# Gated rows by seven products, and lent weight sums, in a two-layer encoder kernel

## The chip, the core and the metric

One core of a Trainium2 chip. The metric is the device time of one execution in microseconds, as the median of several. PE is TensorE, DVE VectorE, ACT ScalarE, POOL GpSimd, SP SyncE; DMA queues are fed by SP and POOL.

## The reference

One inference step of an encoder for a prompt of 512 frames and 8 streams of 16 frames, so 640 tokens, in fp32, with two layers. Each layer is an FFN at half weight, a mixer, and a second FFN:

```
x += 1/2 * SwiGLU_1(RMSNorm(x))
h  = RMSNorm(x);  z = h @ w_in          # conv B | C | V | q | k | v | 2 x 1024 gates
y_c = B * causal_conv3(C * V);  y_a = band attention of q, k, v
m = sigmoid(g_c) * (y_c @ w_conv_out) + sigmoid(g_a) * (y_a @ w_attn_out);  x += m @ w_o
x += 1/2 * SwiGLU_2(RMSNorm(x))
```

The change touches the line with m: y_c and y_a have 512 channels, the gates and m 1024.

## The kernel before

Tokens lie in the free dimension (640, as two halves t1 and t2 of 320), features in partitions, 128 rows at a time. Each fp32 operand is split in a high and a low part (`hi`, `lo`), and a product takes three matmuls per 128 rows: weights hi by x hi, hi by x lo, lo by x hi. ACT makes the high part by a cast, DVE the low one by a subtraction.

**By seven.** Where a weight block of 2 by 2 meets two halves of tokens, seven products are made in place of eight. A *unit* has two weight tiles `ra` and `rb` of 128 x 1024 (n and n + 1 of the stream `wst`) and takes four *slabs* from them, each split into `whi` and `wlo`: the first is `ra` (products 11 and 21), the second a sum `s6` and a sum of `rb`'s halves (N6 and T5), the third sums (T7 and 22), the fourth `rb`'s second half (T4). A product is 12 matmuls of 320 columns. The operands N6, T7, T4 and T5 are sums of the x quarters.

**The stretch.** `outputs` makes, per layer, the gates m = 2 to 15 in pairs (`gate_pair`: one unit for two rows of 128, with banks `qa`, `qb`, `qc`), and the products with `w_conv_out` ("co") and `w_attn_out` ("ao"). Of the latter, the rows 0 to 3 of each are made one by one (`out`: 24 matmuls into `py`), the rows 4 to 7 as one unit (`rows`, banks `ra`, `rb`, `rc`). `mixer_order` gives the order: gates 2, co 0 to 3, gates 4 and 6, co rows 4 to 7, gates 8, ao 0 and 1, gates 10, ao 2 and 3, gates 12 and 14, ao rows 4 to 7, then w_o. PE, DVE and ACT run there in the order in which the code is written.

**Gates.** A gate is scaled by the norm's `rr` (DVE), goes through the sigmoid (ACT), and is multiplied with its output (DVE). `mm` holds the co part and, after the ao part is added, m, which is split for w_o (`m_0hi`, `m_0lo`).

**Lent sums.** `lend_one` lets POOL's queue make a sum in memory: a transfer of half a tile, then a second one that adds. In the units of `lean` (from the third unit of the stretch on) it stands in for a DVE addition.

**Order of preparation.** `prep` makes the casts of a slab on ACT and notes its subtractions, `flush` issues them on DVE, `slab` and `quiet` take the next slab, `ahead` makes the sums of the slab after. There are three buffers for `whi` and three for `wlo`.

Of the kernel before, what the change touches and what calls it, by code (L numbers as in the profile page):

```python
# [194 lines left out]
def trunk(ctx: ExitStack, tc: tile.TileContext, xin, wst, small, pbias, samplebias, kcache, vcache, gfin,  # L197
# [80 lines left out]
    def lend_one(n):  # L278

        z = lent[n] = apart[0].tile([P, CH // 2], F32, tag="one", name=f"one{n}", bufs=2)  # L280
        POOL.dma_start(z, wst[n][:, h1])
        POOL.dma_start(z, wst[n + 1][:, h1], accum_op=ALU.add)
# [19 lines left out]
    def source(i):  # L302
# [3 lines left out]
        if i not in sources:  # L306
# [8 lines left out]
            else:  # L315
# [35 lines left out]
    def prep(i):  # L351
# [8 lines left out]
        o = 0  # L360
        for src, c in parts:
            d = slice(o, o + c.stop - c.start)
            o = d.stop
# [3 lines left out]
    def flush():  # L367
        for lo, src, hi in pending:
            DVE.tensor_tensor(out=lo, in0=src, in1=hi.bitcast(F32), op=ALU.subtract)  # L369
        pending.clear()  # L370
# [3 lines left out]
    def slab(hold=False):  # L374
# [10 lines left out]
        return ready[i], slabs[i]  # L385

# [1110 lines left out]
    def outputs(l, gp, X, st, cs, ycp, yas, sigmoid, gates):  # L1497
# [4 lines left out]
        ycs = [z[:, i] for z in ycp for i in range(2)]  # L1502
        mm = [spare[i // 2][:, i % 2] for i in range(CT)] + ycs
# [7 lines left out]
        lates = []  # L1511

        def due():
            for f in lates:
                f()
            lates.clear()

        def gate_pair(m, at):
            n = f"{l}_{m}"
            pa, pb, pc = (att(f"q{i}{n}")[:, :HT] for i in "abc")  # L1520
            s0 = quiet()
            block(pa, s0, 0, X11, every, True, True)
            ACT.copy(c1, pa)
            due()
            u, g = gates[m], gates[m + 1] = tmp(f"g{n}"), tmp(f"g{n}_1")
            prep(used[0] + 1)
            flush()
            at[0]()
            block(pb, s0, 1, X21, every, True, True)
            add(u[:, t1], pb, c1)  # L1530
            s1 = slab(True)[0]
            flush()
            block(pa, s1, 0, XN6, every, False, True)
            ACT.copy(u2, pa)
            block(pc, s1, 1, XT5, every, True, True)
            ACT.copy(c5, pc)
            at[1]()
            s2 = slab(True)[0]
# [4 lines left out]
            ahead()  # L1543
            at[2]()
            block(pc, s2, 1, X22, every, False, True)
            add(u[:, t2], pc, u2)
            s3 = slab(True)[0]
            DVE.tensor_tensor(out=u, in0=u, in1=rr, op=ALU.mult)
            lates.append(lambda: sigmoid(u, m))
            if m == 2:  # L1550
                for i in range(2):
                    sigmoid(gates[i], i)
            block(pa, s3, 0, XT4, every, False, True)
            DVE.tensor_tensor(out=g[:, t1], in0=pa, in1=rr[:, t1], op=ALU.mult)
            lates.append(lambda: sigmoid(g, m + 1, -1.0))
            flush()

        def parts(pool, tag, name, src):
            hi, lo = (pool.tile([P, T], F32R, tag=f"{tag}{i}", name=f"{name}{i}") for i in ("hi", "lo"))
            split(hi, lo, src)  # L1560
            return hi, lo

        def out(m, y, then=None, post=None):

            due()
            py = acc(f"py{l}_{m}")
            product(py, y)
            if then:
                then()
            g = gates[m]  # L1570
            if m < KT:
                DVE.tensor_tensor(out=halves(mm[m]), in0=two(py), in1=halves(g), op=ALU.mult)
            else:
                DVE.tensor_tensor(out=halves(g), in0=two(py), in1=halves(g), op=ALU.mult)
                add(mm[m - KT], mm[m - KT], g)
            flush()
            if post:
                post()

        yc, ya = [], []  # L1580
        mo = [None] * KT
        srcs = [yas[:, c, :] for c in range(CT)]
        x, moves = {}, []

        def take(y, name, cs, srcs):
            for c in cs:
                y.append(parts(gp, f"y{c}", f"{name}{l}_{c}", srcs[c]))

        def take_even(c):
            y = tuple(gp.tile([P, T], F32R, tag=f"y{c}{i}", name=f"ya{l}_{c}{i}") for i in ("hi", "lo"))  # L1590
            split(*(z[:, t1] for z in y), srcs[c][:, t1])
            ya.append(y)

        def low(lo, z, hi):
            DVE.tensor_tensor(out=lo, in0=z, in1=hi.bitcast(F32), op=ALU.subtract)

        def room(name):
            for k in EXTRA:
                x[name, k] = tuple(gp.tile([P, 2, HT], F32R, tag=f"x{EXTRA.index(k)}{i}",
                                           name=f"x{i}{name}{l}_{EXTRA.index(k)}") for i in ("hi", "lo"))  # L1600

        def minus(out, a):
            DVE.scalar_tensor_tensor(out=out, in0=a, scalar=-1.0, in1=out, op0=ALU.mult, op1=ALU.subtract)

        def mixed(i):

            z = ycp[i].rearrange("p c (a b) -> p (c a) b", a=2)
            e1, e2, o1, o2 = (z[:, k] for k in range(4))
            add(e1, e1, e2, ALU.subtract)
            add(e2, o2, e2, ALU.subtract)  # L1610
            minus(o2, e1)
            minus(o1, o2)
            yield
            for k in EXTRA:
                ACT.copy(x["co", k][0][:, i], z[:, 1 + EXTRA.index(k)])
            yield
            for k in EXTRA:
                hi, lo = (u[:, i] for u in x["co", k])
                low(lo, z[:, 1 + EXTRA.index(k)], hi)
            yield  # L1620
            hi, lo = (u[:, t2] for u in yc[2 * i])
            ACT.copy(hi, e1)
            yield
            low(lo, e1, hi)
            yield

        za = yas.rearrange("p (i c) (a b) -> p i (c a) b", i=2, a=2)

        def mix(n):

            e1, e2, o1, o2 = (za[:, :, k] for k in range(4))
            if n == 0:
                add(e1, e1, e2, ALU.subtract)
            elif n == 1:
                add(e2, o2, e2, ALU.subtract)
            else:
                minus(*((o2, e1) if n == 2 else (o1, o2)))

        def place(k):
            if k == XT5:  # L1640
                return [(*(u[:, t2] for u in ya[2 * i]), za[:, i, 0]) for i in range(2)]
            return [(*x["ao", k], za[:, :, 1 + EXTRA.index(k)])]

        def high(*ks):
            for k in ks:
                for hi, _, z in place(k):
                    ACT.copy(hi, z)

        def rest(*ks):
            for k in ks:  # L1650
                for hi, lo, z in place(k):
                    low(lo, z, hi)

        EXTRA = XT7, XT4, XN6

        def kind(name, i, k):
            if k in EXTRA:
                return tuple(z[:, i] for z in x[name, k])
            hi, lo = (yc if name == "co" else ya)[2 * i + (k in (X21, X22))]
            return tuple(z[:, t2 if k in (X22, XT5) else t1] for z in (hi, lo))  # L1660

        def rows(name, ms, first, mid=None, late=None, end=False, defer=False):

            n = f"{name}{l}_{ms[0]}"
            gs = [gates[m + (KT if name == "ao" else 0)] for m in ms]
# [3 lines left out]
            s1, s2, s5 = stage  # L1669

            def mul(ps, s, half, k, start):
                for u in range(2):
                    for i in range(2):
                        kp = half * NP + 2 * u + i
                        wh, wl = (z[:, kp * P : (kp + 1) * P] for z in s)
                        xh, xl = kind(name, i, k)
# [13 lines left out]
            def moved(r):  # L1690
                for u in range(2):
                    ACT.copy(mm[ms[2 * r + u]], gs[2 * r + u])

            w = quiet()
            mul(a, w, 0, X11, True)
            ACT.copy(s1, two(A))
            due()
            prep(used[0] + 1)
            flush()
            if first:  # L1700
                first()
            mul(b, w, 1, X21, True)
            add(s1, two(B), s1)
            w = slab(True)[0]
            flush()
            mul(a, w, 0, XN6, False)
            ACT.copy(s2, two(A))
# [731 lines left out]
```

## Time and profile before

| what | value |
|---|---|
| median of 3 runs | 2482.03 us (2480.78 to 2482.44) |
| span of the profiled execution | 2479.9 us, 2.1 us below that median |
| busy in the span | PE 99%, DVE 88%, ACT 56%, POOL 13% |
| the stretch of gates and outputs, layer 0 | 635.0 to 774.3 us |
| the same, layer 1 | 1863.5 to 2002.8 us |

The time of an execution is the span from the first to the last instruction and what lies around it. The span of 2479.9 us is that of the profiled execution; no other time of its own is on the page, so the median stands beside it. In a row of the profile, a line, an engine, an operation, and "out<-in" name the tiles with their numbers left out; a row of groups ends with its busy time, the mean of one in ns, and the engine's idle time just before with its cause. In a row of the timeline, the start and the duration come first.

### The profile page before, as it was taken

How to read it: one execution, taken by the hardware profiler on the slowest of the kernel's cores; microseconds unless marked ns; L12 is line 12 of the kernel's file. 1: busy time of each engine (PE TensorE's matmuls, PEld its weight loads, DVE VectorE, ACT ScalarE, POOL GpSimd, SP SyncE). 2: the span in 40 equal slices, each digit the busy share in tenths (PEclk: the TensorE clock that was granted, in tenths of full speed). 3: DMA queues.
4: the chain of work that ended last, by engine and by line, in shares of the span. 5: the costliest groups of instructions: out<-in, count | busy, mean ns of one | idle time of the engine just before them, and what ended most of it. 6: DMA issues, size and time to landing. Idle time of an engine off the chain costs nothing.

```text
span 2479.9 us, 44056 instructions
## 1 busy us (share of the span) xinstructions
PE 2466.4 (99%) x17264; PEld 2414.6 (97%) x17264; DVE 2182.6 (88%) x3644; ACT 1386.7 (56%) x2231; POOL 320.8 (13%) x483
## 2 busy tenths in 40 slices
PE   9999999999999999999999999999999999999999
PEld 8999999889999999999999999998899999999998
DVE  7999998888888899998799999988888889999997
ACT  6555555665555555555665555566655556555555
POOL 0211112211000001111001010121110000111111
PEclk9999999999999999999999999999999999999999
DMA  4443444335344234444334343452453432444444
GB/s 155 128 120 101 124 117 120 114 110 175 102 118 123 93 102 107 112 118 119 109 94 109 110 117 102 117 128 102 138 167 94 119 119 92 108 113 107 112 117 117
DMA packets 113520, 288.16 MB, mean 116 GB/s; under 512 B 12992, under 2 KB 52544, under 8 KB 113312
## 3 DMA queue, kind: packets, MB, share of 16 engines
q1 hardware_dynamic: 69552, 220.10, 27.0%
q0 software_dynamic: 43328, 64.99, 13.8%
q8 instruction: 135, 2.21, 0.4%
q14 instruction: 73, 0.60, 0.1%
q10 hardware_dynamic: 432, 0.25, 0.0%
HBM read 239.48 MB, written 7.94 MB: 100 GB/s over the span
## 4 chain that ended last, share of the span: by engine, by line
PE 91%; DVE 4%; issue 3%; ACT 1%; DMA 1%; DVEq 0%; SPq 0%; ACTq 0%; POOLq 0%
PE pab L459 12%; PE paa L459 10%; PE pcb L459 6%; PE daa L1147 5%; PE dab L1147 5%; PE pca L459 5%; PE po L435 5%; PE qa L459 4%; PE pbb L459 3%; PE dca L1147 3%; PE dcb L1147 2%; PE pba L459 2%; PE ma_cv L459 2%; PE ma_qk L459 2%; PE py L435 2%
## 5 line engine op out<-in xcount | busy, mean ns | idle before, releaser
L364 ACT CAST whi<-raw 128x1024 fp32r<-128x1024 f32 (+1 forms) x578 | 502.3, 874 | 373.4 <-PE pbb L459 46.3
L369 DVE TENSOR_TENSOR wlo<-raw,whi 128x1024 fp32r<-128x1024 f32 (+1 forms) x578 | 577.0, 1001 | 135.4 <-ACT whi L364 131.2
L364 ACT CAST whi<-s 128x1024 fp32r<-128x1024 f32 (+1 forms) x162 | 152.9, 944 | 319.4 <-DVE s L296 113.5
L459 PE MATMUL pab<-xhib,whi 128*128 128x320 f32 x704 | 217.7, 309 | 0.0
L459 PE MATMUL pab<-xhib,wlo 128*128 128x320 f32 x704 | 217.2, 309 | 0.0
L459 PE MATMUL pab<-xlob,whi 128*128 128x320 f32 x704 | 217.2, 309 | 0.0
L459 PE MATMUL paa<-xhia,whi 128*128 128x320 f32 x640 | 197.8, 309 | 0.2 <-DVE ga L296 0.2
L459 PE MATMUL paa<-xhia,wlo 128*128 128x320 f32 x640 | 197.5, 309 | 0.0
L459 PE MATMUL paa<-xloa,whi 128*128 128x320 f32 x640 | 197.5, 309 | 0.0
L369 DVE TENSOR_TENSOR wlo<-s,whi 128x1024 fp32r<-128x1024 f32 (+1 forms) x162 | 176.3, 1088 | 4.0 <-ACT whi L364 4.0
L1169 POOL DMA_DIRECT2D x<-c_a x80 | 69.9, 1021 | 575.9 <-ACT ahia L1051 205.5
L1169 POOL DMA_DIRECT2D x<-c_b x72 | 63.2, 1014 | 583.1 <-ACT ahib L1051 205.4
L459 PEld LDWEIGHTS pab<-xhib,whi 128*128 128x128 f32 x704 | 132.1, 188 | 0.9 <-issue 0.9
L459 PEld LDWEIGHTS pab<-xhib,wlo 128*128 128x128 f32 x704 | 132.1, 188 | 0.0
L459 PEld LDWEIGHTS pab<-xlob,whi 128*128 128x128 f32 x704 | 132.1, 188 | 0.0
L459 PEld LDWEIGHTS paa<-xhia,whi 128*128 128x128 f32 x640 | 120.1, 188 | 1.1 <-DVE ga L296 0.4
L459 PEld LDWEIGHTS paa<-xloa,whi 128*128 128x128 f32 x640 | 120.1, 188 | 0.3 <-DVE xloa L703 0.3
L459 PEld LDWEIGHTS paa<-xhia,wlo 128*128 128x128 f32 x640 | 120.1, 188 | 0.1
L296 DVE TENSOR_TENSOR raw<-s,raw 128x512 f32<-128x512 f32 x162 | 110.7, 683 | 0.0
L459 PE MATMUL pcb<-xhib,wlo 128*128 128x320 f32 x352 | 108.8, 309 | 0.0
L459 PE MATMUL pcb<-xlob,whi 128*128 128x320 f32 x352 | 108.6, 309 | 0.0
L459 PE MATMUL pcb<-xhib,whi 128*128 128x320 f32 x352 | 108.6, 309 | 0.0
(909 smaller groups left out, 8201.3 us busy)
## 6 DMA issues: line engine op xcount, KB each, us to landing
raw<-in_wst SPq DMA_DIRECT2D x375, 512.0 KB, 3.5
x<-c_a POOLq DMA_DIRECT2D x80, 160.0 KB, 4.8
x<-c_b POOLq DMA_DIRECT2D x72, 160.0 KB, 4.2
lent<-in_wst POOLq DMA_DIRECT2D x36, 256.0 KB, 3.7
kc<-in_kcache SPq DMA_DIRECT2D x32, 256.0 KB, 4.8
vc<-in_vcache SPq DMA_DIRECT2D x16, 512.0 KB, 4.3
one<-in_wst POOLq DMA_DIRECT2D x32, 256.0 KB, 4.0
x<-u_a POOLq DMA_DIRECT2D x40, 160.0 KB, 4.1
```

The lines of the kernel that those rows point to most:

```text
L296: DVE.tensor_tensor(out=out, in0=a, in1=b, op=op)
L364: ACT.copy(hi[:, d], src[:, c])
L369: DVE.tensor_tensor(out=lo, in0=src, in1=hi.bitcast(F32), op=ALU.subtract)
L435: PE.matmul(ps[:, a, :HT], w, x[a] if isinstance(x, tuple) else x[:, a * HT : (a + 1) * HT], start=first and j == 0 and not seeded, stop=l ...
L459: PE.matmul(ps, a, b, start=start and kp == 0 and j == 0, stop=stop and kp == NP - 1 and j == 2, skip_group_check=True)
L1147: PE.matmul(ps[u], w, y, start=start and i == 0 and j == 0, stop=i == 1 and j == 2, skip_group_check=True)
L1169: POOL.dma_start(x[ms[2 * u + r]][:, cols], z[:, u], accum_op=ALU.add)
```

## The change

The rows 0 to 3 of co and of ao become units of seven products as well. The new order is gates 2 and 4, co rows 0 to 3, gates 6, co rows 4 to 7, gates 8 and 10, ao rows 0 to 3, gates 12 and 14, ao rows 4 to 7: eleven units in a row. Besides:

- The lent sum is now that of `rb`'s two halves, which the second slab of a unit needs (for s6 and as its T5 half). DVE makes the sum of `ra` and `rb` for the third slab in its place, and that slab is cast and split whole, as 1024 columns.
- The sum s6 is made by `ahead` before the T7 product of the unit ahead.
- The rms scaling of a pair's first gate is put off (`off`, `due`) to the next unit; sigmoids and copies are a list of `tasks` that the units take from one by one.
- `Mixed` makes all operands of co and ao by quarters, its steps spread over the two gate units ahead and the unit itself.
- In `rows`, the products go 11, T5, N6, 21, T7, 22, T4; from the second unit of a layer on the first product is copied into the bank of 21, in place of an addition. Some gated products are put off to the next unit (`put_off`).

```diff
@@ mixer_order
-    out += gates[:2] + [("co", m) for m in range(4)] + gates[2:4] + [("rows", ("co", (4, 5, 6, 7)))]
-    for i in range(2):
-        out += [gates[4 + i], ("ao", 2 * i), ("ao", 2 * i + 1)]
-    out += gates[6:] + [("rows", ("ao", (4, 5, 6, 7)))]
+    rows = [("rows", (name, ms)) for name in ("co", "ao") for ms in ((0, 1, 2, 3), (4, 5, 6, 7))]
+    out += gates[:3] + rows[:1] + gates[3:4] + rows[1:2] + gates[4:6] + rows[2:3] + gates[6:] + rows[3:]
@@ lend_one
-        POOL.dma_start(z, wst[n][:, h1])
-        POOL.dma_start(z, wst[n + 1][:, h1], accum_op=ALU.add)
+        POOL.dma_start(z, wst[n + 1][:, h1])
+        POOL.dma_start(z, wst[n + 1][:, h2], accum_op=ALU.add)
@@ source, second slab of a lean unit
-                    flush()
                     st = sums[n] = spool[0].tile([P, CH // 2], F32, tag="s6", name=f"s6_{n}", bufs=1)
-                    add(rb[:, h1], rb[:, h1], rb[:, h2])
-                    add(st, rb[:, h1], ra[:, h1])
-                    sources[i] = [(st, h1), (rb, h1)]
+                    add(st, lent[n], ra[:, h1])
+                    sources[i] = [(st, h1), (lent.pop(n), h1)]
@@ source, third slab
-                    if kind == "gu" and n not in lean:
+                    if kind == "gu" and n not in lean or kind == "mix" and n in lean:
                         add(ra[:, h1], ra[:, h1], rb[:, h1])
                     add(ra[:, h2], sums.pop(n)[:, h1], ra[:, h2])
-                    sources[i] = [(lent.pop(n), h1), (ra, h2)] if n in lean else [(ra, whole)]
+                    sources[i] = [(lent.pop(n), h1), (ra, h2)] if n in lent else [(ra, whole)]
@@ outputs, the sequence
-        gate_pair(2, [none, none, lambda: take(yc, "yc", range(CT), ycs)])
...
-        rows("ao", (4, 5, 6, 7), None, lambda: given(1, 3), None, True)
+        gate_pair(2, joined(one, task("b", "e")))
+        gate_pair(4, joined(due_, two_, task("b")), True)
+        rows(yc, (0, 1, 2, 3), joined(due_, three, task("b", "c", "d")), 3)
+        gate_pair(6, joined(due_, {"a": [ya.begin]}, task("b", "c", "d")), True)
+        rows(yc, (4, 5, 6, 7), joined(due_, task("b", "c", "d")), 1)
+        one, two_, three = ya.steps(True)
+        gate_pair(8, joined(due_, one, task("b", "d")))
+        gate_pair(10, joined(due_, two_, task("b")), True)
+        rows(ya, (0, 1, 2, 3), joined(due_, three, task("b", "c", "d")), 1)
+        gate_pair(12, joined({"s": [lambda: total(0)], "a": [lambda: total(1)]}, due_,
+                             {"a": [lambda: total(2, 3)]}))
+        gate_pair(14, joined(due_, task("b", "e"), {"c": [lambda: (begun(*range(4)), given(0, 2))]}), True)
+        rows(ya, (4, 5, 6, 7), joined(due_, {"a": [lambda: given(1, 3)]}, task("b", "c")))
```

How the queues stand, at two places. First, DVE in the unit of gate 4 of layer 0, before; `g0_4` and `g0_4_1` are the pair's two rows, `raw98` and `raw99` the next unit's weights, `rrm0` the norm:

```order
L296 TENSOR_TENSOR g0_4_7613<-qb0_4_7598,capsm0_4819 128x320
L369 TENSOR_TENSOR wlo179_7638<-raw97_7523,whi179_7637 128x512
L1595 TENSOR_TENSOR yc0_0lo_7397<-yc0_0_4821,yc0_0hi_7396 128x320
L1595 TENSOR_TENSOR yc0_2lo_7405<-yc0_1_4822,yc0_2hi_7404 128x320
L296 TENSOR_TENSOR g0_4_1_7614<-qa0_4_7597,c50_4831 128x320
L1541 TENSOR_TENSOR g0_4_1_7614<-g0_4_1_7614,rrm0_4820 128x320
L369 TENSOR_TENSOR wlo180_7672<-raw98_7669,whi180_7671 128x1024
```

The same place in the change; `mm0_1` holds gate 2, `yc0` the conv output's quarters, `y4co0` the splits of their sums, `one96` the lent sum:

```order
L294 TENSOR_TENSOR g0_4_0_7486<-qb0_4_7471,capsm0_4819 128x320
L366 TENSOR_TENSOR wlo177_7508<-raw95_7415,whi177_7507 128x512
L1574 TENSOR_TENSOR mm0_1_7302<-mm0_1_7302,rrm0_4820 128x640
L1614 TENSOR_TENSOR y4co0_0lo_7317<-yc0_0_4821,y4co0_0hi_7316 128x320
L1614 TENSOR_TENSOR y4co0_1lo_7319<-yc0_1_4822,y4co0_1hi_7318 128x320
L1623 SCALAR_TENSOR_TENSOR yc0_1_4822<-yc0_1_4822 128x320
L1623 SCALAR_TENSOR_TENSOR yc0_0_4821<-yc0_0_4821 128x320 x2
L1623 SCALAR_TENSOR_TENSOR yc0_1_4822<-yc0_1_4822 128x320 x2
L294 TENSOR_TENSOR s6_96_7559<-one96_7417,raw96_7549 128x512
L294 TENSOR_TENSOR g0_4_1_7487<-qa0_4_7470,c50_4831 128x320
L1562 TENSOR_TENSOR g0_4_1_7487<-g0_4_1_7487,rrm0_4820 128x320
L366 TENSOR_TENSOR wlo178_7552<-raw96_7549,whi178_7551 128x1024
```

Between the adds of `qb` and `qa` there stand now the scaling of the gate before, five sums of quarters and s6.

Second, the co rows 4 to 7 of layer 0, DVE and then ACT, from the sums for the third slab to the split of the fourth. Before, DVE:

```order
L296 TENSOR_TENSOR raw100_7800<-s6_100_7825,raw100_7800 128x512
L369 TENSOR_TENSOR wlo186_7882<-one100_7691,whi186_7881 128x512
L369 TENSOR_TENSOR wlo186_7882<-raw100_7800,whi186_7881 128x512
L296 TENSOR_TENSOR capsm0_4819<-rbco0_4_7861,capsm0_4819 128x640
L369 TENSOR_TENSOR wlo187_7901<-raw101_7820,whi187_7900 128x512
```

and ACT:

```order
L1354 ACTIVATE g0_6_7748<-g0_6_7748,sm_73 128x640
L1354 ACTIVATE g0_6_1_7749<-g0_6_1_7749,sm_73 128x640
L364 CAST whi186_7881<-one100_7691 128x512
L364 CAST whi186_7881<-raw100_7800 128x512
L364 CAST whi187_7900<-raw101_7820 128x512
```

In the change, DVE (`yc0_1` holds gates 6 and 7 there):

```order
L294 TENSOR_TENSOR raw100_7819<-raw100_7819,raw101_7824 128x512
L294 TENSOR_TENSOR raw100_7819<-s6_100_7829,raw100_7819 128x512
L366 TENSOR_TENSOR wlo188_7899<-raw100_7819,whi188_7898 128x1024
L1574 TENSOR_TENSOR yc0_1_4822<-yc0_1_4822,rrm0_4820 128x640
L366 TENSOR_TENSOR wlo189_7945<-raw101_7824,whi189_7944 128x512
```

and ACT:

```order
L361 CAST whi188_7898<-raw100_7819 128x1024
L1695 COPY rs0_1_7304<-rcco0_4_0_7881 128x320
L1695 COPY rs0_1_7304<-rcco0_4_1_7882 128x320
L1355 ACTIVATE yc0_1_4822<-yc0_1_4822,sm_73 128x640
L1698 COPY rs0_0_7303<-raco0_4_7880 128x640
L1355 ACTIVATE yc0_1_4822<-yc0_1_4822,sm_73 128x640
L361 CAST whi189_7944<-raw101_7824 128x512
```

The split of the third slab stands directly behind its second sum, and the cast for the fourth behind two sigmoids, of which the first reads what DVE scales just ahead.

More of the change, by code (lines that the diff above doesn't have):

```diff
@@ L1542, in gate_pair @@
             flush()
-            ahead()
-            at[2]()
+            call("d")
             block(pc, s2, 1, X22, every, False, True)
             add(u[:, t2], pc, u2)
[L1547 to L1552, printed above, removed]
+            s3 = quiet()
+            following(rows_next)
+            if rows_next:
+                flush(1)
@@ L1580, in outputs @@
[L1580 to L1625, printed above, removed]
@@ L1666, in rows @@
+        seeded = [False]
+        def rows(y, ms, at={}, put_off=0):
+            n = f"{y.name}{l}_{ms[0]}"
+            co = y.name == "co"
+            gs = [gates[m + (0 if co else KT)] for m in ms]
             B, A = (acc(f"r{i}{n}") for i in "ba")
@@ L1688, in gated @@
                                                  op0=ALU.mult, op1=ALU.mult)
-            def moved(r):
-                for u in range(2):
-                    ACT.copy(mm[ms[2 * r + u]], gs[2 * r + u])
             w = quiet()
[L1695 to L1698, printed above, removed]
+            call("s")
+            mul(a, w, 0, "11", True)
+            ACT.copy(two(B) if seed else s1, two(A))
+            following()
             flush()
-            if first:
-                first()
@@ L1702, in rows @@
[L1702 to L1707, printed above, removed]
-            gated(0, [s1[:, u] for u in range(2)], t1)
-            if mid:
-                mid()
-            mul(c, w, 1, XT5, True)
+            call("a")
+            w1 = quiet()
+            mul(c, w1, 1, "T5", True)
             for u in range(2):
                 ACT.copy(s5[:, u], c[u])
-            w = slab(True)[0]
@@ L1715, in rows @@
-            mul(a, w, 0, XT7, False)
+            call("b")
+            mul(a, w1, 0, "N6", False)
+            ACT.copy(s2, two(A))
+            call("c")
+            mul(b, w, 1, "21", not seed)
+            following()
+            if not seed:
+                add(s1, two(B), s1)
+            flush()
+            w = quiet()
+            following()
+            gated(0, b if seed else [s1[:, u] for u in range(2)], t1)
+            ahead()
+            call("d")
+            mul(a, w, 0, "T7", False)
@@ L1716, in rows @@
             add(s5, two(A), s5)
             flush()
-            ahead()
-            if defer:
-                moves.append(lambda: gated(1, [s5[:, u] for u in range(2)], t2, -1.0))
-            else:
-                gated(1, [s5[:, u] for u in range(2)], t2, -1.0)
-            if late:
-                late()
-            mul(c, w, 1, X22, False)
+            left = [lambda: gated(1, [s5[:, u] for u in range(2)], t2, -1.0),
+                    lambda: gated(0, [s2[:, u] for u in range(2)], t2), lambda: gated(1, a, t1, -1.0)]
@@ L1726, in rows @@
+            if not put_off:
+                left.pop(0)()
+            mul(c, w, 1, "22", False)
             for u in range(2):
                 add(s2[:, u], c[u], s2[:, u])
-            w = slab(True)[0]
-            gated(0, [s2[:, u] for u in range(2)], t2)
-            mul(a, w, 0, XT4, False)
-            if not end:
-                flush()
-            gated(1, a, t1, -1.0)
-            if name == "co":
-                lates.append(lambda: moved(0))
-                moves.append(lambda: moved(1))
@@ L1737, in rows @@
-            if end:
-                flush()
+            w = quiet()
+            following()
+            if not put_off:
+                left.pop(0)()
+            mul(a, w, 0, "T4", False)
+            flush()
+            while len(left) > put_off:
+                left.pop(0)()
+            off.extend(left)
+            if co:
+                tasks.extend(lambda u=u: ACT.copy(mm[ms[u]], gs[u]) for u in range(2))
+            call("e")
+        mo = [None] * KT
         def total(*ms):
@@ L1777, in outputs, with quarters, joined @@
-        rows("ao", (4, 5, 6, 7), None, lambda: given(1, 3), None, True)
+        def quarters(z):
+            return z.rearrange("p c (a b) -> p (c a) b", a=2)
+        def joined(*zs):
+            return {k: [f for z in zs for f in z.get(k, ())] for k in "sabcde"}
+        due_, task = {"a": [due]}, lambda *ks: {k: [some()] for k in ks}
+        yc = Mixed("co", [quarters(z) for z in ycp])
+        ya = Mixed("ao", [quarters(yas[:, 2 * i : 2 * i + 2]) for i in range(2)])
+        one, two_, three = yc.steps()
```

195 lines of the change are left out of this document (103 added, 92 removed).

## The prediction

> **What bounds the kernel now.** I read the page's shares first, then its chain, then the stretch of each mixer that the change rewrites.
>
> ```profile
> span 2479.9 us, 44056 instructions
> PE 2466.4 (99%) x17264; PEld 2414.6 (97%) x17264; DVE 2182.6 (88%) x3644; ACT 1386.7 (56%) x2231; POOL 320.8 (13%) x483
> PE 91%; DVE 4%; issue 3%; ACT 1%; DMA 1%; DVEq 0%; SPq 0%; ACTq 0%; POOLq 0%
> ```
>
> PE is the bound: 99% busy, 91% of the chain. A matmul that goes away is worth its step, and a wait of PE costs its full length. The stretch of gates and outputs is 635.0 to 774.3 us in layer 0, and the same in layer 1; by engine (PE, PEld, DVE, ACT, POOL):
>
> ```profile
> 635.00:774.30 139.30, 139.25 (x950) 138.95 (x949) 120.73 (x195) 79.91 (x133) 8.60 (x12) 1.00 0.36 106
> 1863.50:2002.80 139.30, 139.25 (x950) 138.94 (x949) 120.64 (x195) 79.82 (x133) 8.64 (x12) 1.00 0.35 107
> ```
>
> PE has no gap at the full clock (1.00). DVE is busy 120.7 of 139.3 us: it has 18.6 us to spare, and that is what the change spends. DVE's groups there (busy, mean ns, idle before and its cause):
>
> ```profile
> L369 DVE TENSOR_TENSOR wlo<-raw,whi 128x512 fp32r<-128x512 f32 x26 | 17.8, 685 | 0.5
> L369 DVE TENSOR_TENSOR wlo<-raw,whi 128x1024 fp32r<-128x1024 f32 x14 | 17.1, 1219 | 0.9 <-ACT whi L364 0.9
> L369 DVE TENSOR_TENSOR wlo<-one,whi 128x512 fp32r<-128x512 f32 x8 | 5.5, 690 | 2.5 <-ACT whi L364 2.5
> L296 DVE TENSOR_TENSOR g<-qa,c 128x320 f32<-128x320 f32 x7 | 3.4, 491 | 12.4 <-PE qa L459 12.4
> ```
>
> 12.4 of the 18.6 us are waits for PE: DVE is ahead. 2.5 us are waits for ACT's cast of a weight half that was summed just before.
>
> **The steps of the engines.** A plain output is 24 matmuls (12 rows of x2); its first and the next output's first:
>
> ```profile
> 650.83 0.46 PE L435 MATMUL py<-yc_0hi,whi 128*128 128x320 f32 x2
> 654.35 0.46 PE L435 MATMUL py<-yc_0hi,whi 128*128 128x320 f32 x2
> ```
>
> 3.52 us by 24 is 0.1465 us a matmul; a product of 12 takes 1.758, a unit of seven products 12.31. DVE's instructions overlap, so a queue is added by starts, not by durations:
>
> ```profile
> 752.60 0.68 DVE L369 TENSOR_TENSOR wlo<-s,whi 128x512 fp32r<-128x512 f32 x1
> 753.20 0.68 DVE L369 TENSOR_TENSOR wlo<-raw,whi 128x512 fp32r<-128x512 f32 x1
> 769.29 0.89 DVE L1685 TENSOR_TENSOR g<-capsm,g 128x320 f32<-128x320 f32 x2
> 770.09 0.82 DVE L236 TENSOR_TENSOR m_1lo<-mm,m_1hi 128x640 fp32r<-128x640 f32 x1
> 770.82 0.82 DVE L236 TENSOR_TENSOR m_3lo<-mm,m_3hi 128x640 fp32r<-128x640 f32 x1
> 772.29 1.22 DVE L369 TENSOR_TENSOR wlo<-raw,whi 128x1024 fp32r<-128x1024 f32 x1
> 773.43 0.89 DVE L1687 SCALAR_TENSOR_TENSOR g<-rs,g 128x320 f32<-128x320 f32 x2
> ```
>
> The steps are 0.60 us (512 wide), 0.40 (320: two in 0.80), 0.735 (640) and 1.135 (1024); each start lies 0.08 before the end of the one before it. The Trainium skill, "VectorE: DVE Perf Modes", speaks against this change in its section "The DRAIN you can't avoid": the pipe has to empty before the next op starts, which makes a step the whole duration. Its section "Two Vector instructions with no wait between them" lets an instruction that is not held start earlier, and the trace, with its 0.08, agrees with that one. The sum goes by the steps; by whole durations DVE would need some 18 us more per mixer, a rival below.
>
> What a late weight costs PE:
>
> ```profile
> 752.97 0.31 PE L459 MATMUL qa<-tlo,whi 128*128 128x320 f32 x1
> 753.33 0.41 PE L459 MATMUL qa<-thi,wlo 128*128 128x320 f32 x1
> 753.59 0.31 PE L459 MATMUL qa<-thi,whi 128*128 128x320 f32 x1
> ```
>
> The third matmul of a product is the first that reads a wlo. The wlo above (752.60) ends at 753.28; the matmul starts at 753.33 instead of 753.12 and its successor 0.11 later still. So PE follows DVE one for one, plus 0.1.
>
> **What is removed.** Per mixer eight plain outputs of 24 matmuls (192) become two more seven-product units of 84 (168): 24 matmuls, 3.52 us, all on the path. The 0.3 us wait at 753.33 goes too, as its sum is made sooner. Together 3.8 per mixer, 7.6 in all.
>
> **What is added on DVE.** From the order, per mixer from the last sum ahead of gate 2 to the last split of mm: 69 instructions of 512 become 65, 48 TENSOR_TENSOR and 2 SCALAR_TENSOR_TENSOR of 640 become 36, 73 of 320 become 103, 15 of 1024 become 23. In steps: -4 x 0.605 - 14 x 0.737 + 30 x 0.402 + 8 x 1.135 = +8.4 us, 125.0 to 133.4, while PE's stretch shrinks to 135.8.
>
> **A new wait, once a unit.** Before, the third slab of a unit came in two halves, and the split of the lent half stood between the sum of the other and its split:
>
> ```profile
> 676.73 0.68 DVE L296 TENSOR_TENSOR raw<-s,raw 128x512 f32<-128x512 f32 x1
> 678.08 0.69 DVE L369 TENSOR_TENSOR wlo<-one,whi 128x512 fp32r<-128x512 f32 x1 [0.67 <-ACT whi L364]
> ```
>
> Now two sums are followed at once by the split of the whole slab, which waits for ACT's cast of 1024:
>
> ```profile
> L364 ACT CAST whi<-raw 128x1024 fp32r<-128x1024 f32 x15 | 15.8, 1053 | 2.9 <-PE qc L459 1.4 <-PE rcao L1678 1.4 <-DVE raw L296 0.2
> L364 ACT CAST whi<-raw 128x512 fp32r<-128x512 f32 x26 | 15.5, 620 | 5.9 <-DVE raw L296 5.5 <-PE qb L459 0.2
> L1354 ACT ACTIVATE g<-g,sm 128x640 f32<-128x640 f32 x16 | 12.4, 826 | 5.5 <-DVE g L1548 5.5
> L1707 ACT COPY rs<-raao 128x640 f32<-128x640 f32 x1 | 0.7, 694 | 0.0
> ```
>
> A sum ends 0.08 after its step, a handover takes 0.03 (753.28 to 753.33 above is one), the cast 1.05, another 0.03: DVE stands 1.2 us, ten times per mixer, and everything in its queue behind it too. In the second co unit there is one more: the split of the fourth slab stands behind a cast that ACT makes after two sigmoids and a copy, and the first sigmoid needs DVE's rms product just ahead. 0.1 + 0.73 + 0.6 + 0.73 + 0.65 = 2.8 us (the durations above, less 0.1 where ACT's next overlaps).
>
> **DVE's queue walked against PE.** Each leg runs from one point where both meet to the next.
> - Leg A, from the T4 product of gate 2 (DVE must wait for it, 0.27 after its end) to the T7 product of the first co unit: 32 instructions (15 x 0.402, 10 x 0.605, 4 x 0.737, 3 x 1.135) = 18.4, two waits of 1.2, 0.1 for a dependent pair, 0.1 for the result: 21.3. PE has 11 products, 19.3, and 0.6 more until it reads the last operand: 1.4 late.
> - Leg B, to the first product of gate 10: 66 instructions = 37.7, three waits of 1.2, the 2.8, pairs 0.2: 44.3. PE has 24 products, 42.2, and the deadlines of the two ends differ by 0.3, so 41.9: 2.4 late.
> - Leg C, to T7 of the first ao unit: 33 = 18.8, 2.4, 0.1, against 19.6: 1.7.
> - Leg D, to gate 14: 29 = 17.2, 1.2, 0.1, against 17.3: 1.1.
> - Leg E, to the last ao unit: 16 = 10.1, 1.2, a wait of 1.9 for the cast of mm behind ACT's copy of T5, 0.1, against 12.3: 1.0.
> - Leg F, to the first w_o product: 15 = 9.9, 1.2, 1.4 for the cast behind two sigmoids, against 12.3: 0.1. The tail, where the last gated products and splits of mm precede two products of w_o: 2.0. Before, this tail has no room either, so lateness there is passed on whole: the row below ends at 782.41, and PE, which is through T4 at 774.3, reads it after 8 blocks of 0.88, one more and two matmuls, at 782.5.
>
> ```profile
> 781.59 0.82 DVE L236 TENSOR_TENSOR m_5lo<-yc,m_5hi 128x640 fp32r<-128x640 f32 x1
> ```
>
> Sum 9.7, and 0.1 for about eight restarts, where part of the tail's may overlap: 10.0 us per mixer.
>
> **Edits that I cost at nothing.** Two more units are lent (10 for 8, two 256 KB transfers each):
>
> ```profile
> 666.95 0.57 POOL L281 DMA_DIRECT2D one<-in_wst  x1 [41.98 <-DVE wlo L369]
> 670.63 0.86 POOL L282 DMA_DIRECT2D one<-in_wst  x1 [3.11 <-DMA one<-in_wst]
> DMA to landing us min/median/max: 2.9/4.0/5.9
> ```
>
> Two transfers take some 8 us, at most 12; with two buffers they start when the unit before has read its own, and the new sum comes some 20 us later. Without that cover each us late is a us of DVE. The seeding copy from PSUM to PSUM has no row; the nearest, PSUM to SBUF, is 0.69. I take that, between 0.4 (a 320 copy) and 1.4 (double); it has two products, 3.5 us, until its bank is read, so neither end costs PE. The three adds that it saves are in the count above. ACT has 59 us free in the stretch; only the chains above count.
>
> **Sum.** 2 x (10.0 - 3.8) = +12.4 us on the profiled span: 2479.9 to 2492.3. The runs' median, 2482.03, lies 2.1 above the span; so 2494.4. Bounds of the unknown: leg B's chain and the ten waits are each either there or not.
>
> **Rivals.**
> - DVE keeps up (faster). Its place is the wait between sum and split, ten times; its price 1.2. At nothing, legs A to F end on time and only the tail's 1 us is left: 2482.0 - 7.6 + 2 = 2476.4. It decides from about 0.5 us a wait down. For it: the trace has only 0.67 there at most. Against: there a split of another half stood between, and now the order has nothing. 0.10.
> - The 2.8 us chain is covered. Leg B is then on time, the rest sums to about 6.5: 2482.0 + 2 x 2.7 = 2487.4. For it: ACT could have run its sigmoids earlier if DVE's product came earlier; against: the order has DVE's product just before. 0.20.
> - PSUM banks come free late: a late DVE also reads old banks late, and PE's next product waits for them. Some 2 us per mixer more: 2498.5. 0.08.
> - The lent sums come late, so that the step to transfers fails: 1 to 3 us per mixer more: 2500. 0.03.
> - DVE's instructions do not overlap: 222 x 0.08 = 18 us more per mixer, 2530. The starts above speak against it. 0.01. The Trainium skill's drain section, above, would give this time.
>
> **Chances.** The forecast has 0.58. No change that can be told is within 0.2%, 2477.1 to 2487.0. Faster 0.09 (most of the first rival), same 0.17 (the rest of it, half of the second and a little of the first case's low end), slower 0.74. The range of 2480 to 2502 leaves out the first rival and the lowest of the second (0.13), and the last ones (0.06).
>
> **What would show it.** PE's plain py products gone and 672 matmuls at the gated rows' line; DVE's split of the summed slab with 1 us or more of idle, released by ACT, ten times per mixer; PE waiting for DVE at T7 of the first unit of co and of ao and at gate 10. Wrong if DVE still waits for PE some 10 us per stretch, or PE has no gap.

## The result, and the profile after

The changed kernel takes 2493.86 us (median of 4, 2493.71 to 2495.5) against 2481.69 us before (median of 4, one execution more than in the table above); the ratio is 1.0051, 95% interval 1.0037 to 1.0065. It is slower by 12.2 us, and by 11.7 us in span (2479.9 to 2491.6). The page of the changed kernel (span, busy times, the chain by engine):

```profile
span 2491.6 us, 44040 instructions
PE 2465.9 (99%) x17216; PEld 2407.7 (97%) x17216; DVE 2194.4 (88%) x3684; ACT 1400.4 (56%) x2243; POOL 327.0 (13%) x491
PE 86%; DVE 9%; ACT 2%; issue 2%; DMA 1%; SPq 0%; DVEq 0%; ACTq 0%; POOLq 0%
```

The shares of busy time say almost nothing: PE is at 99% as before. The chain does: PE falls from 91% to 86%, DVE rises from 4% to 9%. The stretch begins and ends with these rows of PE's timeline:

```profile
634.71 0.31 PE L460 MATMUL qa<-hhim,whi 128*128 128x320 f32 x1
...
780.00 0.45 PE L436 MATMUL po<-m_0hi,whi 128*128 128x320 f32 x2
```

It takes 145.3 us for 139.3. It holds 77 products (11 units of 7) at 1.758, 135.4 us, so PE stands for 9.9 us (9.6 in layer 1, counted alike). Before, PE was busy for 139.25 of 139.30 us and no wait of it is listed. DVE's waits in layer 0 (engine, line and tile, what it waited for; then us in total, how often, the longest), and the single waits in its timeline (start, duration, in brackets the idle time just before and who ended it), of the changed kernel:

```profile
DVE wlo L366 <- ACT whi L361: 18.2, 14, 2.7
DVE m_0lo L234 <- ACT m_0hi L233: 1.8, 1, 1.8
```

```profile
651.62 1.22 DVE L366 TENSOR_TENSOR wlo<-raw,whi 128x1024 fp32r<-128x1024 f32 x1 [1.17 <-ACT whi L361]
665.19 1.23 DVE L366 TENSOR_TENSOR wlo<-raw,whi 128x1024 fp32r<-128x1024 f32 x1 [1.11 <-ACT whi L361]
...
694.76 0.69 DVE L366 TENSOR_TENSOR wlo<-raw,whi 128x512 fp32r<-128x512 f32 x1 [2.72 <-ACT whi L361]
...
771.12 1.23 DVE L366 TENSOR_TENSOR wlo<-raw,whi 128x1024 fp32r<-128x1024 f32 x1 [1.18 <-ACT whi L361]
775.80 0.69 DVE L366 TENSOR_TENSOR wlo<-raw,whi 128x512 fp32r<-128x512 f32 x1 [1.25 <-ACT whi L361]
```

DVE had waited 12.4 us for PE's `qa` in the stretch; now no such wait is left, and in the stretch it waits 18.0 us for ACT's casts: ten times 1.11 to 1.18 us between sum and split (once in every unit from the second, that of gate 4, on), once 2.72, once 1.84, once 1.25, once 0.57. The row of 18.2 begins at 630 us and so takes in a wait of 1.99 ahead of the stretch, which the kernel before has too; so do the rows of DVE's waits for casts below. Where PE stands is in PE's waits over the same time:

```profile
PE qa L460 <- DVE g L294: 4.3, 5, 1.3
PE raco L1673 <- DVE rs L294: 0.8, 2, 0.4
PE raao L1673 <- ACT rs L1698: 0.4, 1, 0.4
PE raao L1673 <- DVE y4ao_0lo L1614: 0.3, 1, 0.3
PE raco L1673 <- DVE y4co_0lo L1614: 0.3, 1, 0.3
```

The rows sum to 6.1 us of the 9.9: a row counts from the end of the matmul before, 0.31 after its start, though the next one usually starts 0.147 after it; a matmul that waited runs 0.1 longer; and the shortest pauses have no row. The largest is not a weight or an operand that comes late. Product T4 adds into the bank that T7 has left, and DVE must have read T7 from it. One of the five, at gate 8, on DVE and on PE:

```profile
709.91 0.49 DVE L1623 SCALAR_TENSOR_TENSOR ya<-ya 128x320 f32<-128x320 f32 x1
710.31 0.69 DVE L294 TENSOR_TENSOR s<-one,raw 128x512 f32<-128x512 f32 x1
710.91 0.49 DVE L294 TENSOR_TENSOR g<-qa,c 128x320 f32<-128x320 f32 x1
```

```profile
711.46 0.42 PE L460 MATMUL qa<-thi,whi 128*128 128x320 f32 x1 [1.18 <-DVE g L294]
```

T7 itself is long done; DVE comes to its read at 710.91 since its queue ahead is full, and PE starts T4 at 711.46, 0.06 after the read ends.

### The profile page after: what moved, and what is told of

It is laid out like the page before. It is cut to its first block, busy times and chain, and to the rows that moved or that the text cites. A ratio compares the mean times of both kernels' runs of the same rounds, so it can differ in the third digit from the quotient of the medians.

```text
span 2491.6 us, 44040 instructions
## 1 busy us (share of the span) xinstructions
PE 2465.9 (99%) x17216; PEld 2407.7 (97%) x17216; DVE 2194.4 (88%) x3684; ACT 1400.4 (56%) x2243; POOL 327.0 (13%) x491
## 4 chain that ended last, share of the span: by engine, by line
PE 86%; DVE 9%; ACT 2%; issue 2%; DMA 1%; SPq 0%; DVEq 0%; ACTq 0%; POOLq 0%
PE pab L460 12%; PE paa L460 11%; PE pcb L460 6%; PE daa L1148 6%; PE pca L460 5%; PE dab L1148 5%; PE po L436 5%; PE pbb L460 3%; PE dca L1148 3%; PE pba L460 3%; DVE wlo L366 3%; PE dcb L1148 2%; PE ma_cv L460 2%; PE ma_qk L460 2%; PE pv L1832 2%; PE qa L460 2%
## 5 line engine op out<-in xcount | busy, mean ns | idle before, releaser
L366 DVE TENSOR_TENSOR wlo<-raw,whi 128x512 fp32r<-128x512 f32 (+1 forms) x566 | 578.2, 1024 | 166.2 <-ACT whi L361 162.0
L361 ACT CAST whi<-raw 128x512 fp32r<-128x512 f32 (+1 forms) x566 | 501.6, 892 | 378.1 <-DVE raw L294 49.2
```

The source lines that it names most:

```text
L361: ACT.copy(hi[:, d], src[:, c])
```

## The experiments

All times are medians. The kernel before ran beside each set of experiments on the same chip, with medians of 2481.10 to 2481.13, so these times can be set side by side; beside the changed kernel it had 2481.69, so a difference from the changed kernel carries some 0.6 us. "PE stands" is the sum over the products of layer 0's stretch of what each takes beyond 1.758 us, by the starts of their first matmuls (the rounding of the step makes 10.0 here of the 9.9 above).

| run | us | ratio to before, 95% | PE stands, layer 0 |
|---|---|---|---|
| changed kernel | 2493.86 | 1.0051 (1.0037 to 1.0065) | 10.0 |
| e1_halves | 2479.52 | 0.9994 (0.9985 to 1.0002) | 2.8 |
| e2_lent_as_before | 2489.24 | 1.0033 (1.0021 to 1.0046) | 8.2 |
| e3_before_new_lent | 2484.15 | 1.0012 (1.0003 to 1.0022) | |
| e4_no_scaling | 2484.41 | 1.0014 (1.0005 to 1.0023) | 5.2 |
| e5_sum_late | 2493.93 | 1.0052 (1.0040 to 1.0065) | 10.0 |
| e6_chain | 2491.84 | 1.0044 (1.0030 to 1.0057) | 8.2 |
| e7_lent_before_sum_late | 2478.64 | 0.9990 (0.9981 to 0.9999) | 2.4 |
| e8_best | 2476.10 | 0.9978 (0.9970 to 0.9987) | 1.4 |
| e9_lent_before_all | 2477.82 | 0.9985 (0.9976 to 0.9994) | 2.0 |
| e10_halves_sum_late | 2477.41 | 0.9985 (0.9976 to 0.9994) | 1.9 |
| e11_scaling_at_once | 2493.71 | 1.0050 (1.0036 to 1.0063) | 10.6 |

**e1_halves: the wait between sum and split taken away.**

```diff
-sources[i] = [(lent.pop(n), h1), (ra, h2)] if n in lent else [(ra, whole)]
+sources[i] = ([(lent.pop(n), h1), (ra, h2)] if n in lent else
+              [(ra, h1), (ra, h2)] if kind == "mix" and n in lean else [(ra, whole)])
```

> The changed kernel with one thing different: the third slab of a gate or output unit, the one whose 1024 columns are summed just before, is cast and split as two halves of 512, so that DVE need not stand from its second sum to the end of the cast of all 1024. Theory (DVE's chain sum, cast, split puts DVE back 1.2 us ten times per mixer, and that lateness is what PE pays): the wait shrinks to 0.1 to 0.3 us, DVE keeps up in most legs, and the time falls by 6 to 9 us per mixer: 2476 to 2482 us. Rival (it is DVE's sheer work, or the order of its reads of PSUM ahead of T4, that PE pays): within 2 us of the changed kernel, 2492 to 2495.

Measured 2479.52, within the theory's range: 14.3 us under the changed kernel. ACT casts the first half while DVE makes the second sum, here in the first co unit:

```profile
661.01 0.68 DVE L294 TENSOR_TENSOR raw<-raw,raw 128x512 f32<-128x512 f32 x1
661.61 0.68 DVE L294 TENSOR_TENSOR raw<-s,raw 128x512 f32<-128x512 f32 x1
661.73 1.23 ACT L362 CAST whi<-raw 128x512 fp32r<-128x512 f32 x2 [0.18 <-DVE raw L294]
662.38 1.29 DVE L367 TENSOR_TENSOR wlo<-raw,whi 128x512 fp32r<-128x512 f32 x2
```

DVE's and PE's waits in layer 0 with it:

```profile
DVE wlo L367 <- ACT whi L362: 8.7, 8, 2.7
DVE m_0lo L234 <- ACT m_0hi L233: 2.1, 1, 2.1
...
PE qa L461 <- DVE g L294: 0.9, 3, 0.4
PE raco L1674 <- DVE rs L294: 0.4, 2, 0.2
```

DVE's wait for casts falls by 9.5 us, PE's standing by 7.2 per layer, 14.3 in both. DVE has more instructions than in the changed kernel, not fewer (3704 for 3684). So the loss needs the wait, ten times per mixer; the count of DVE's instructions alone does not make it. With the wait gone the loss is gone too, but no gain is shown: the interval of the ratio, 0.9985 to 1.0002, takes in 1. That DVE's own time counts as well, where its queue is full, is what e4_no_scaling shows below.

**e2_lent_as_before: the other weight sum lent again.**

```diff
 def lend_one(n):
-    POOL.dma_start(z, wst[n + 1][:, h1])
-    POOL.dma_start(z, wst[n + 1][:, h2], accum_op=ALU.add)
+    POOL.dma_start(z, wst[n][:, h1])
+    POOL.dma_start(z, wst[n + 1][:, h1], accum_op=ALU.add)
 ...
-add(st, lent[n], ra[:, h1])
-sources[i] = [(st, h1), (lent.pop(n), h1)]
+add(rb[:, h1], rb[:, h1], rb[:, h2])
+add(st, rb[:, h1], ra[:, h1])
+sources[i] = [(st, h1), (rb, h1)]
 ...
-if kind == "gu" and n not in lean or kind == "mix" and n in lean:
+if kind == "gu" and n not in lean:
```

> The changed kernel with the weight sums made as before: the transfers make the first half of the third slab, DVE the two sums of the second slab. DVE's count of sums is the same, its split of the third slab is two of 512 for one of 1024. Theory (the wait between sum and split): it shrinks from 1.2 to the 0.3 us that it has before the change, so the time is near that of the halves, 2477 to 2484. Rival (which sum is lent has no weight; the added 8 us of DVE steps are what counts): 2491 to 2496.

Measured 2489.24: neither. The theory of the wait alone fails here, since the order matters too: `ahead` now puts two sums ahead of DVE's read of T7's bank. The timeline of the three engines at the end of the first co unit and in the next gate shows what that starts:

```profile
670.14 0.69 DVE L294 TENSOR_TENSOR raw<-raw 128x512 f32<-128x512 f32 x1
670.86 0.69 DVE L294 TENSOR_TENSOR s<-raw,raw 128x512 f32<-128x512 f32 x1
671.47 0.81 DVE L294 TENSOR_TENSOR rs<-raco,rs 128x640 f32<-128x640 f32 x1
...
672.43 0.39 PE L1674 MATMUL raco<-y4co_0hi,whi 128*128 128x320 f32 x1 [0.95 <-DVE rs L294]
...
676.23 0.43 ACT L1542 COPY capsm<-qa 128x320 f32<-128x320 f32 x1 [3.43 <-PE qa L461]
676.55 0.62 ACT L362 CAST whi<-one 128x512 fp32r<-128x512 f32 x1
...
677.20 0.69 DVE L367 TENSOR_TENSOR wlo<-one,whi 128x512 fp32r<-128x512 f32 x1 [1.19 <-ACT whi L362]
```

PE stands 0.95 us for the read. Being late, it ends the next gate's first product late; ACT's copy of that stands ahead of ACT's cast of the next slab, so that comes late too; and DVE, which had been late, now waits 1.19 for the cast and is late once more. At this place PE's lateness comes back to DVE through ACT's queue.

**e7_lent_before_sum_late: the same with these sums behind the read.** In `gate_pair` (and alike in `rows`, where `ahead()` goes behind `add(s5, two(A), s5)` and its `flush()`):

```diff
 following()
-ahead()
 block(pa, s2, 0, XT7, every, False, True)
 add(g[:, t2], pa, c5)
 DVE.tensor_tensor(out=g[:, t2], in0=g[:, t2], in1=rr[:, t2], op=ALU.mult)
 flush()
+ahead()
```

> The kernel of the run with the weight sums as before, and beside it the sums for N6 behind DVE's read of T7's bank. That run missed its forecast: it came out at 2489, with DVE's waits for casts down from 18 to 12 us, but it has two sums instead of one ahead of T7's read, 1.2 us, and PE waits 1 us there. Theory A (these two sums ahead of T7's read are what kept it slow): 2479 to 2484 us. Theory B (the 4 us more of DVE's busy time that the trace shows, and the waits left, are what kept it slow): 2487 to 2490.

Measured 2478.64, 10.6 under e2_lent_as_before, a little better than theory A had it. At the place above the read stands first now, PE does not stand there, and the loop is not entered; in the timeline, the split follows ACT's copy and cast without a wait of DVE:

```profile
668.96 0.82 DVE L294 TENSOR_TENSOR rs<-raco,rs 128x640 f32<-128x640 f32 x1
...
673.83 0.43 ACT L1542 COPY capsm<-qa 128x320 f32<-128x320 f32 x1 [0.34 <-PE qa L461]
674.15 0.62 ACT L362 CAST whi<-one 128x512 fp32r<-128x512 f32 x1
...
674.82 0.69 DVE L367 TENSOR_TENSOR wlo<-one,whi 128x512 fp32r<-128x512 f32 x1
```

**e5_sum_late: that edit alone, on the changed kernel.** 

> The changed kernel with one part undone: the sum for N6 stands behind DVE's read of T7's bank again, not ahead of it, in the gate units and in the output units. In the changed kernel PE waits mostly at T4, which adds to the bank that this read must have left. Theory 1 (DVE's queue is full, so an instruction moved by one place changes where PE waits, but not how much in all): 2490 to 2494 us. Theory 2 (PE pays for what stands ahead of T7's read at each T4, 0.6 us at five gate pairs and a part of it at the output units): 6 to 8 us less, 2485 to 2488.

Measured 2493.93, against 2493.86: nothing. PE stands for 10.0 us as before the edit, at other places; its waits in layer 0:

```profile
PE qa L460 <- DVE g L294: 2.7, 3, 1.2
PE raao L1673 <- ACT rs L1698: 1.4, 2, 1.0
PE raco L1673 <- ACT rs L1698: 1.0, 2, 0.6
PE raco L1673 <- DVE y4co_0lo L1614: 0.4, 1, 0.4
PE raao L1673 <- DVE y4ao_0lo L1614: 0.4, 1, 0.4
```

T4's wait falls from 4.3 to 2.7 us and others take it up. In the stretch of the changed kernel DVE is busy or waits for ACT's casts all the time but for a few tenths of a us (126.8 and 18.0 of 145.3 us). With such a queue, the row of waits tells where PE meets the lateness, not what makes it.

**e10_halves_sum_late: that edit on e1_halves.** 

> The changed kernel with the summed slab in two halves and N6's sum behind T7's read, nothing else. In the changed kernel the place of that sum made no difference (2493.93 against 2493.86), with the weight sums as before it made 10.6 us. Theory (the place of the sum counts only where DVE has room otherwise: there the read of T7's bank is what PE waits for, and the wait is not made good, since ACT's next cast then stands behind a copy that waits for PE): the halves alone leave 2.6 us of waits at T4 per mixer, most of which goes: 2475 to 2478. Rival (no effect here either): 2479 to 2481.

Measured 2477.41, 2.1 under e1_halves, and PE stands for 1.9 us instead of 2.8: the place of the sum counts again once the ten waits are gone. The difference is small: the intervals of the two ratios overlap, the single times (2476.61 to 2478.79, and 2478.30 to 2481.82) barely do. In the three pairs the same edit is worth 0 (queue full), 2.1 and 10.6 us.

**e3_before_new_lent: the new weight sum alone, in the kernel before.** It takes `lend_one` and the lines of `source` from the changed kernel and nothing else (the reverse of the diff of e2_lent_as_before, with the whole slab). 

> The kernel before with one part of the change alone: the other weight sum is made by the transfers, and the third slab is summed whole and split whole. DVE then stands 1.2 us once a unit here too, eight times per mixer, but it has 12 us of waits for PE in the stretch. Theory: the wait is mostly covered, 2481 to 2486 us, so the new sum alone is not what costs; it costs only together with the fuller DVE queue. Rival (the new wait costs PE whatever else DVE does): 8 x 1.2 x 2 = 19 us more, 2495 to 2501.

Measured 2484.15, within the theory's range: 3.0 us, not 19. DVE's waits in layer 0:

```profile
DVE wlo L368 <- ACT whi L363: 12.6, 11, 2.0
DVE g L296 <- PE qa L458: 8.4, 5, 2.6
```

The waits for casts are there, but 8.4 us of waits for PE are still there too: DVE makes most of the waits for casts good. The wait costs its full price only where the queue has no room left.

**e4_no_scaling: 5.2 us less of DVE per mixer.** The line `off.append(lambda: DVE.tensor_tensor(out=u, in0=u, in1=rr, op=ALU.mult))` is left out. 

> The changed kernel without the rms scaling of the first gate of each pair (left out of the computation), which takes seven instructions of 640 columns, 7 x 0.74 = 5.2 us, out of DVE's queue per mixer and touches neither the waits between sum and split nor the lent sums. Theory (DVE is the bound in the stretch, so its time is worth its length there): PE's waits fall by 3 to 5 us per mixer, 2484 to 2488. Rival (PE pays only for single chains, not for DVE's total): 2491 to 2495.

Measured 2484.41, 9.5 under the changed kernel; 2 x 5.2 would be 10.4. DVE's time in the stretch is worth nearly its length to PE, though DVE's waits for casts are not shorter than in the changed kernel (19.0 for 18.2 us):

```profile
DVE wlo L366 <- ACT whi L361: 19.0, 15, 2.5
```

**e11_scaling_at_once: the rms scaling in its own unit again.** The same line's product stands right behind `s3 = quiet()`. 

> The changed kernel with one part undone: the gates' rms scaling stands where it was, behind the read of product 22 of its own unit and ahead of T4's read, and not a unit later. The count of DVE's instructions is the same. Theory (DVE's queue is full; the scaling takes its 0.74 us wherever it stands, but the sigmoids of the second co unit no longer wait for it, which takes about 0.7 out of the 2.7 us chain): 2491 to 2494 us. Rival (0.74 ahead of T4's read puts the chain of weight sums behind it back, and PE pays it again in each of seven units): 2496 to 2503.

Measured 2493.71, as the theory had it. The wait of 2.72 in the second co unit falls to 1.97, but others grow (that of 1.25 to 1.75) and PE stands no less. Putting the scaling off neither cost nor brought anything that can be told.

**e6_chain: the two sigmoids of the second co unit behind the cast.**

```diff
-rows(yc, (4, 5, 6, 7), joined(due_, task("b", "c", "d")), 1)
+rows(yc, (4, 5, 6, 7), joined(due_, {"d": [some(2)]}), 1)
```

> The changed kernel with the two sigmoids in the second co unit put behind the cast of the fourth slab, so that DVE's split of that slab no longer waits 2.7 us behind rms product, sigmoid, sigmoid, copy and cast. Theory (a wait of DVE is paid by PE one for one up to the next place where both meet, gate 8): the wait falls to 0.5 us or less, PE's 2.3 us in this leg fall to about 0.4, and the time by 2 x 1.9: 2489 to 2491 us. Rival (DVE only waits at the next place instead, for the sigmoids that are later now, or for the next cast): 2492 to 2495.

Measured 2491.84 (2490.12 to 2493.00), in a gap between the two: some 2 us of the 3.8. The wait did not fall to 0.5:

```profile
692.45 0.69 DVE L366 TENSOR_TENSOR wlo<-raw,whi 128x512 fp32r<-128x512 f32 x1 [1.06 <-ACT whi L361]
```

The cast now stands behind ACT's copy of product N6 (691.21, which waits for PE), so 1.66 of the 2.72 are won, and PE stands for 1.8 us less in layer 0: one for one. The trace is that of the fastest execution, 2490.12; two layers of 1.8 would be 3.5 us, the median has 2.0. The times of this kernel differ by 2.9 us, so the size stays rough.

**e9_lent_before_all and e8_best.** e9 is e7_lent_before_sum_late with the edit of e6_chain and, in gate 14, the first casts of m ahead of ACT's copy of T5 (`given(0, 2)` called at "b", not "c"). e8 is e10_halves_sum_late with these two.

> The weight sums as before the change, N6's sums behind T7's read, and beside these the two sigmoids of the second co unit behind the cast and the first casts of the output sums ahead of ACT's copy of T5. In the run without the last two DVE has 2.7 and 1.8 us of waits for these casts, and PE 2.4 us of waits per mixer are left. Theory (what PE still waits is DVE's lateness from these chains): 2475 to 2477 us. Rival (these chains are covered by now, as PE waits at none of the places just behind them): 2478 to 2479.5.

> Four edits to the changed kernel together: the summed slab in two halves, N6's sum behind T7's read, the two sigmoids of the second co unit behind the cast, and the first casts of the output sums ahead of ACT's copy of T5 (DVE waits 1.8 to 2.1 us for them otherwise). With the halves alone 2.6 us of PE's waits per mixer were left. Theory (all of them are DVE's lateness, from these causes): most of it goes, 2474 to 2477 us, below both kernels. Rival (DVE's queue is full, and the moves only shift the waits): 2478 to 2481.

e9: 2477.82 against 2478.64, between its two forecasts, and the times overlap; unclear. It is a weak test, since the two waits did not go: in its trace the one in the second co unit falls from 2.7 to 1.49, the one for `m_0` from 1.8 to 1.51 (e8 has the same two), and PE stands for 2.0 us instead of 2.4. e8: 2476.10, 1.3 under e10_halves_sum_late and 5.0 under the kernel before (ratio 0.9978, 0.9970 to 0.9987). Its stretch of 140 us (PE, PEld, DVE, ACT, POOL):

```profile
635.00:775.00 140.00, 139.59 (x947) 138.54 (x946) 131.05 (x230) 84.40 (x144) 11.98 (x17) 1.00 0.41 118
```

The changed kernel's same 140 us:

```profile
635.00:775.00 140.00, 133.88 (x891) 130.30 (x890) 122.29 (x207) 80.82 (x132) 11.46 (x16) 1.00 0.39 110
```

DVE does more in the same time, since it stands less, and PE has 56 matmuls more behind it. Of the 7.6 us that were to be removed 5.0 arrive; for most of the rest PE still stands (1.4 us in layer 0).

## Why the prediction was right, point by point

It said 2494.4 us, 12.4 more than before; measured were 2493.86, 12.2 more (11.7 in span). The mechanism was that of the text: DVE's queue loses its slack to the added work and the ten waits between sum and split, and PE pays.

- **Removed.** 48 matmuls fewer (17264 to 17216), so 24 per mixer: as worked out; and the output units' line (L1673) has 672, as named.
- **The new wait.** 1.2 us were given, ten times per mixer: 1.11 to 1.18, ten times. The chain in the second co unit: 2.8 given, 2.72 measured; the cast of m: 1.9 and 1.84; the last unit's cast: 1.4 and 1.25. e1_halves shows that the ten decide: without them the loss is gone. (The 0.03 given for a handover was read too short: the rows that it names, 753.28 and 753.33, are 0.05 apart. In a sum of 1.2 it does not count.)
- **The overlap of DVE's instructions.** The forecast went by steps from start to start, 0.08 shorter than the durations. The rows at gate 8 above go on so (709.91, 710.31, 710.91 for durations of 0.49 and 0.69). Steps of a whole duration would by the estimate on record have made 2530; the measured time excludes that for these operations. The Trainium skill, "VectorE: DVE Perf Modes", section "The DRAIN you can't avoid", which the forecast set against the change, itself lets a next op that is not held start earlier; the starts here agree with that.
- **The legs.** Their sum was 10.0 us per mixer; PE stands for 9.9. The single terms were not as good. By the starts of the products in layer 0: leg A 1.8 (given 1.4), B 3.0 (2.4), C 1.6 (1.7), D 1.6 (1.1), E 1.3 (1.0), F 0.7 (0.1), the tail 0.1 (2.0). The legs were 2.3 us too short together, and the tail 1.9 too long. So part of the near hit is luck: two errors that cancel. Of the legs' shortfall, 0.33 us lie ahead of leg A's start, at gate 2's own T4, and in leg F the listed wait of PE is for ACT's copy `rs` (0.35), not for DVE; the rest was not traced.
- **The tail.** "Lateness there is passed on whole" was the wrong step, and its 2.0 us had no rows behind them. The end of DVE's split of `m_5` is the deadline that was given:

```profile
787.24 0.82 DVE L234 TENSOR_TENSOR m_5lo<-yc,m_5hi 128x640 fp32r<-128x640 f32 x1
```

It ends at 788.06. PE starts w_o at 780.00 and reads the split at 788.41, so it is just in time, as before: the split ends 8.06 us after that start, 8.11 before the change. So DVE is no later against PE here than it was: PE had stood for the lateness of the units ahead already, in the units.
- **Where PE stands.** T7 of the first co and ao units is right (the two `y4` rows in PE's waits). Gate 10 is not: PE stands for that lateness already one product earlier, at T4 of gate 8 (711.46, 1.18 us; at T4 of gate 10 it is 0.40), and T4, where most of the waits are, the text had not named at all. As a sum that did no harm.
- **The rivals.** That DVE keeps up is out in this kernel; e1_halves comes near it (2479.5, where the rival's 2476.4 had also the other chains covered). That the 2.8 us chain is covered: it is there, and by e6_chain the 1.66 us of it that went were worth about 2 us of the time (3.5 by the trace); what all of it is worth was not measured. The sum of this rival does not come out: without leg B the terms leave 7.3, not 6.5, which makes about 2489, not 2487.4. That banks come free late: they do, but in the changed kernel as the place of the lateness, not as an addition of 2 us per mixer; e5_sum_late moves it without a change of time. That lent sums come late: no, DVE's sums that read them have no idle time ahead:

```profile
L294 DVE TENSOR_TENSOR s<-one,raw 128x512 f32<-128x512 f32 x10 | 6.9, 688 | 0.0
```

- **The seeding copy** was taken at 0.69 us and at no cost to PE; its row in ACT's timeline, and no wait of PE for it:

```profile
688.34 0.68 ACT L1688 COPY rbco<-raco 128x640 f32<-128x640 f32 x1 [2.48 <-PE raco L1673]
```

Open are the sizes of the small steps: what the sigmoids' place is worth (2 us with times 2.9 apart), and whether the cast of m ahead of T5's copy brings anything by itself, which was not run alone. The 1.4 us per mixer for which PE still stands in e8_best were not followed up; in its trace they lie mostly in the first ao unit and in gates 12 and 14.

## What to carry to other kernels

An engine with 13% of free time in a stretch can still be the one that sets the end, if an edit makes it stand for another engine's result with nothing of its own to put in between. Where a sum is followed by a cast elsewhere and by an instruction on its result, split the work in two, so that the second sum covers the first cast; here that was worth 14.3 us. Before believing a row of waits, ask whether the engine named there has free time: if not, the row shows where lateness is met, and moving one instruction moves the row alone.

## What the runs showed that had not been expected

- In these kernels a product that adds into a bank waited for the read of the bank's last result, though that product was long done: 4.3 us per layer of PE's listed waits were for DVE's reads of T7 in the gate units (up to 1.3 us each), 0.6 for operands. In e2_lent_as_before, two sums of 0.6 us ahead of this read cost 10.6 us per execution, as e7_lent_before_sum_late shows.
- Lateness can go round: PE late by 0.95 us, ACT's copy of PE's product late, the cast behind it late, DVE standing 1.19 us for it. The same edit was worth 0, 2.1 or 10.6 us, by what else filled the queue; that this loop makes up the 10.6 is argued from one place, not shown.
